# Long attention branch A: high-query by low-key products in two 64-row matmuls, one on each half of the array

## The chip, the cores and the metric

The kernel runs on one core of one Trainium2 chip. The metric is the device time of one execution in microseconds (us); lower is better. Three executions of the kernel before took 2085.16, 2086.23 and 2087.42 us (median 2086.23). TensorE is called PE for its matmuls and PEld for the loads of the stationary operand (the weights); DVE is VectorE, ACT ScalarE, POOL GpSimd, and SP is the queue from which most DMAs are issued.

## The reference, cut to what matters

One encoder layer is applied to two sequences, one of 512 tokens and one of 1024. Its token mixer has two branches. Branch A is grouped-query attention: 8 query heads of 64 values, in two groups of four heads, each group with one key and one value head:

```
def block(qi):
    s = jnp.einsum('bqkgd,bskd->bkgqs', qi, k, preferred_element_type=jnp.float32) * scale
    p = jax.nn.softmax(s, axis=-1)
    return jnp.einsum('bkgqs,bskd->bqkgd', p.astype(v.dtype), v)
```

Everything is float32: `q` and `k` are normalised and rotated before, the outputs of both branches are gated, added and multiplied by `w_out`, and an MLP follows.

## The kernel before

**Numbers in two parts.** PE multiplies values in the type `F32R`, which keeps fewer bits than float32. Every operand is therefore kept as a high part (a copy in `F32R`) and a low part (what the copy left off). A product is taken in three matmuls: high by high, low by high, high by low.

**Scores of branch A.** A head has only 64 rows to contract over, half of the array's 128. The kernel uses the other half for the low part: for an even head, `qT[0]` holds the high queries on partitions 0 to 63 and the low queries on 64 to 127; for an odd head, `qT[1]` has them the other way round. `kT[:, 0]` holds the high keys on both halves, `kT[:, 1]` the low keys on both. One matmul of `qT` (128 rows, 128 queries) with `kT[:, 0]` thus gives high by high plus low by high, and one with `kT[:, 1]` adds high by low (and low by low). A matmul covers 512 keys. The short sequence (512 tokens, `NB` = 1) needs two matmuls for a tile of 128 queries, the long one (1024 tokens, `NB` = 2) four, two for each half of the keys: lines 812 and 813, in `s_tile`.

**What follows a score tile.** DVE takes the maximum of the tile from PSUM (L815), ACT the exponential (L824), and the tile's PSUM buffer (`big`, two of them, each two banks of 512 columns) is free again. In the long sequence a head has eight tiles (`u` is head and block of 512 queries, `j` the tile in it). The block `qb` = 0 is transposed on PE (L859) and cut into high and low parts by ACT and DVE; the block `qb` = 1 is transposed by DVE, written to DRAM (`turn_a`, L878), fetched back in quarters (`fetch_a`, L903) and cut by ACT and POOL (`cut_a`). Then PE multiplies with the values (L846, L847). `fill.pull(n)` puts matmuls of the gates (`gate`, tile `gps`) between.

**Stages and order.** The short sequence comes first. For each sequence and each group `g` there is a stage phR (projections, norms, rotation; `heads_t` makes `qT` and `kT` from a transposed tile in PSUM) and a stage phA (the attention); then follow branch B, the projections, and the MLP of both sequences. For the long sequence phA runs from about 440 to 531 us (g = 0) and from 620 to 710 us (g = 1) of the profile. The code is recorded in program order, and a scheduler sets the order of each engine's instructions; the order shown below is the one that it gave.

**Buffers.** `qT`, `kT` and the values `vhl` come from one pool of equal slots of 2 x 1024 numbers for each partition; in the long sequence `vhl` fills half of its slot.

Of the kernel before, what the change touches and what calls it, by code (L numbers as in the profile page):

```python
# [18 lines left out]
P = 128  # L19
D = 1024  # L20
NC8 = D // P
HD = 64
# [39 lines left out]
def encoder(ctx: ExitStack, tc: tile.TileContext, xs, outs, w):  # L62
# [24 lines left out]
    def slot(shape, dt, name, left=False):  # L87
        return (s8l if left else s8r).tile(shape, dt, tag="s8", name=name)
# [336 lines left out]
    def run(tr, nxt, first):  # L425
# [120 lines left out]
        for g in range(2):  # L546
            with phase(f"phR{N}_{g}") as ph:
# [79 lines left out]
                    wv = load_v(g, lambda s_, d_, n_: ph.tile(s_, d_, tag="wv", name=n_, bufs=2), first and fresh, held)  # L627
                qT = [slot([P, 2, T], F32R, f"qT{N}_{g}_{i}") for i in range(2)]
                kT = slot([P, 2, T], F32R, f"kT{N}_{g}")
                vhl = slot([P, NT, P], F32R, f"vhl{N}_{g}")  # L630
                rr_of = {}

                def next_norm(tt):
# [3 lines left out]
                def heads_t(tt):  # L637
                    nm = f"{N}_{g}_{tt}"
                    pt = big(f"pq{nm}")[:, :384].rearrange("p (b q) -> p b q", q=P)
                    rrf = rr_of.pop(tt).rearrange("p h d -> p (h d)")  # L640
                    for b in range(3):
                        nc.tensor.transpose(pt[:, b, :], rrf[:, b * P : (b + 1) * P], ident)
                    ts_ = slice(tt * P, (tt + 1) * P)

                    half = (slice(0, HD), slice(HD, P))
                    nc.scalar.activation(kT[:, 0, ts_], pt[:, 2, :], AF.Copy)
                    for e in range(2):
                        op = nc.scalar.activation(qT[e][half[e], :, ts_], pt[half[e], 0:2, :], AF.Copy)
                    nc.vector.tensor_tensor(kT[:, 1, ts_], pt[:, 2, :], kT[:, 0, ts_].bitcast(F32), op=ALU.subtract)
                    for e in range(2):  # L650
                        nc.vector.tensor_tensor(
                            qT[e][half[1 - e], :, ts_],
                            pt[half[e], 0:2, :],
                            qT[e][half[e], :, ts_].bitcast(F32),
                            op=ALU.subtract,
                        )
                    return op.ins
# [142 lines left out]
            with phase(f"phA{N}_{g}") as ph:  # L800
# [3 lines left out]
                def s_tile(u, j):  # L804
                    h, qb = u
                    nm = f"{N}_{g}_{h}_{qb}_{j}"
                    q0 = (qb * 4 + j) * P
                    lhs = qT[h % 2][:, h // 2, q0 : q0 + P]
                    s = big(f"s{nm}")[:, :T]
                    for kb in range(NB):  # L810
                        ks = slice(kb * 512, kb * 512 + 512)
                        nc.tensor.matmul(s[:, ks], lhs, kT[:, 0, ks], start=True, stop=False)
                        nc.tensor.matmul(s[:, ks], lhs, kT[:, 1, ks], start=False, stop=True)  # L813
                    nm_ = sml.tile([P, 1], F32, tag="nm", name=f"nm{nm}")
                    nc.vector.tensor_reduce(nm_, s, axis=AX.X, op=ALU.max, negate=True)  # L815
                    p = ph.tile([P, T], F32, tag="P", name=f"p{nm}", bufs=8)
                    if j == 0:
                        L4[u] = ph.tile([P, 4], F32, tag="l4", name=f"l{nm}", bufs=4)
                    l = L4[u][:, j : j + 1]
                    to, of = p, s  # L820
                    if NB == 2 and qb == 1:
                        to = p.rearrange("p (b k i) -> p k b i", b=4, i=32)
                        of = s.rearrange("p (k i b) -> p k b i", b=4, i=32)
                    op = nc.scalar.activation(to, of, AF.Exp, bias=nm_, accum_out=l)  # L824
                    PP[u, j] = p
                    if j == 3:
                        rl = ph.tile([P, 32], F32, tag="r4", name=f"rl{nm}", bufs=1)
                        nc.gpsimd.memset(rl, 0.0)
                        nc.vector.reciprocal(rl[:, 0:4], L4.pop(u))
                        nc.vector.transpose(rl, rl)  # L830
                        rd[u] = dram.tile([P, 32], F32, name=f"rd{nm}")
                        nc.gpsimd.dma_start(rd[u], rl)
                    return op.ins

                o_of, rb_of = {}, {}

# [53 lines left out]
                def fetch_a(u, i):  # L890
                    nm = f"{N}_{g}_{u[0]}_{i}"
                    if i < 3:
                        hl = slot([P, 2, 16, 64], F32R, f"hq{nm}")
                        hi, lo = hl[:, 0], hl[:, 1]
                    else:
                        hi, lo = (
                            ph.tile([P, T], F32, tag="P", name=f"hq{nm}_{e}", bufs=8)
                            .bitcast(F32R)
                            .rearrange("p (a w) -> p a w", w=64)
                            for e in range(2)  # L900
                        )
                    src = PD[u].rearrange("t (a i) (b w) -> i b (t a) w", i=32, b=4)[:, :, :, 64 * i : 64 * i + 64]
                    nc.sync.dma_start(lo.bitcast(F32), src)  # L903
                    quarter[u, i] = hi, lo
# [7 lines left out]
                if NB == 2:  # L912
                    subtract[0] = nc.gpsimd
                    for u in ((0, 1), (0, 0)):
                        for j in range(4):
                            last_exp[:] = [step_s(u, j)]
                            fill.pull(1)
                    for i in range(3):
                        fetch_a((0, 1), i)
                    for h in range(4):  # L920
                        u, nn, nd = (h, 1), (h + 1, 0), (h + 1, 1)
                        for kc in range(NT):
                            t_chunk((h, 0), kc)
                            if h == 0 and kc in (0, 2, 4, 6):
                                step_s(nd, kc // 2)
                            elif 0 < h < 3 and kc in (1, 4):
                                step_s(nd, 2 + kc // 4)
                            if kc == 0 and h > 0:
                                fetch_a(u, 2)
                            if kc == 2:  # L930
                                fetch_a(u, 3)
                            if kc in (1, 2, 5):
                                cut_a(u, kc // 2)
                            fill.pull(1 if kc % 4 < 3 else 0)
                            next_pv()
                        for kc in range(NT):
                            if kc == 0:
                                cut_a(u, 3)
                            if h < 3 and kc in (0, 1, 2, 4):
                                step_s(nn, min(kc, 3))  # L940
                            if h < 2 and kc in (5, 7):
                                step_s((h + 2, 1), kc // 7)
                            hi, lo = (t[:, :, kc % 2 * 32 : kc % 2 * 32 + 32] for t in quarter[u, kc // 2])
                            queue.append((u, kc, hi, lo))
                            fill.pull(0 if kc in (1, 4) else 1)
                            next_pv()
                            if h < 3 and kc in (4, 6):
                                fetch_a(nd, kc // 2 - 2)
                else:
                    for j in range(4):  # L950
                        ends = s_tile(units[0], j)
                        last_exp[:] = [ends]
                        fill.pull(2)
                    for ui, u in enumerate(units):
                        h, qb = u
                        if first:
                            bias_row(g * 4 + ui)
                            if g == 0 and ui == 1:
                                early["a"] = load_a(1)
                            if g == 0 and ui == 2:  # L960
                                early["v"] = load_v(1, slot)
                        nxt_u = units[ui + 1] if ui + 1 < len(units) else None
                        sdone = 0
                        for kc in range(NT):
                            t_chunk(u, kc)
                            if nxt_u is not None:
                                while sdone < 4 and kc >= (0, 0, 1, 2)[sdone]:
                                    s_tile(nxt_u, sdone)
                                    sdone += 1

                            fill.pull(1)
                            next_pv()
# [1149 lines left out]
```

## Time and profile before

| what | value |
|---|---|
| time, median of three runs | 2086.23 us |
| time of the profiled execution | 2086.59 us |
| its span, first to last instruction | 2084.8 us |
| granted TensorE clock | 0.999 |
| PE busy | 2065.9 us |
| DVE busy | 1457.2 us |
| ACT busy | 1141.5 us |
| POOL busy | 449.9 us |

The profiled execution took 1.8 us more than its span. Busy times overlap, since the engines run beside each other. The end of a matmul is modelled: matmuls are pipelined, and a row's length is not the distance to the next matmul. What a stage can give up is read from the starts of matmuls that follow each other.

### The profile page before, as it was taken

What the parts mean: (1) busy time and instruction counts of PE and PEld (TensorE: products, weight loads), DVE (VectorE), ACT (ScalarE), POOL (GpSimd) and SP (SyncE); (2) the same over time, 40 slices, a digit from 0 to 9 for tenths busy, and PEclk for the clock granted to TensorE, in tenths of its full rate; (3) what the DMA queues carried; (4) which work ended last, traced back from release to release, by engine and by line L of the source; (5) the groups of instructions that cost most, each with busy time, mean ns of one, the idle gap of its engine ahead of it and who ended that gap; (6) DMA issues with size and microseconds to landing.
All of it is one profiled execution on the core that took longest, in us unless ns stands there. A gap on an engine that the chain in (4) does not pass through costs nothing. (4 is left out here: it accounts for less than half of the span.)

```text
span 2084.8 us, 31252 instructions
## 1 busy us (share of the span) xinstructions
PE 2065.9 (99%) x10615; PEld 1811.7 (87%) x10615; DVE 1457.2 (70%) x2691; ACT 1141.5 (55%) x2455; POOL 449.9 (22%) x556
## 2 busy tenths in 40 slices
PE   9999999999999999999999999999999999999998
PEld 8888878987898788888888999999999988888887
DVE  6665786778458647778845877777777777669563
ACT  6664663767557735566413665665655634334442
POOL 2324310328625744443002000011000000000000
PEclk9999999999999999999999999999999999999999
DMA  6536567558528867766544656587444899788461
GB/s 195 149 110 185 170 186 250 186 150 230 149 65 231 211 188 211 216 216 216 190 164 167 200 177 196 160 257 198 162 143 158 300 336 340 223 278 277 151 212 61
DMA packets 407910, 409.99 MB, mean 197 GB/s; under 512 B 98367, under 2 KB 334919, under 8 KB 407751
## 3 DMA queue, kind: packets, MB, share of 16 engines
q1 hardware_dynamic: 369879, 340.90, 53.0%
q10 hardware_dynamic: 27648, 40.22, 5.7%
q0 software_dynamic: 10224, 26.88, 5.1%
q8 instruction: 84, 1.38, 0.3%
q14 instruction: 75, 0.61, 0.1%
HBM read 294.21 MB, written 114.49 MB: 196 GB/s over the span
## 5 line engine op out<-in xcount | busy, mean ns | idle before, releaser
L216 PE MATMUL dn<-wd,ah 128*128 128x512 f32 x1248 | 384.2, 389 | 0.0
L216 PEld LDWEIGHTS dn<-wd,ah 128*128 128x128 f32 x1248 | 234.2, 188 | 48.7
L216 PE MATMUL dn<-wd,al 128*128 128x512 f32 x624 | 242.8, 389 | 0.0
L1596 ACT ACTIVATE ah<-ar 128x512 fp32r<-128x512 f32 x168 | 104.6, 628 | 208.6 <-PE dn L216 195.3
L216 PE MATMUL gpss<-xs_0h,w_gs 128*128 128x512 f32 x512 | 185.9, 399 | 0.0
L1597 DVE TENSOR_TENSOR al<-ar,ah 128x512 fp32r<-128x512 f32 x168 | 114.3, 686 | 81.5 <-ACT ah L1596 70.4
L216 PE MATMUL ud<-B,A 128*128 128x384 f32 x768 | 143.7, 334 | 0.7 <-DVE c L1714 0.7
L216 PE MATMUL uc<-B,A 128*128 128x384 f32 x768 | 143.7, 334 | 0.0
L216 PE MATMUL ua<-B,A 128*128 128x384 f32 x768 | 138.8, 334 | 0.0
L216 PEld LDWEIGHTS dn<-wd,al 128*128 128x128 f32 x624 | 117.1, 188 | 24.2
L216 PEld LDWEIGHTS ud<-B,A 128*128 128x128 f32 x768 | 134.0, 188 | 1.0 <-DVE c L1714 1.0
L216 PEld LDWEIGHTS uc<-B,A 128*128 128x128 f32 x768 | 134.1, 188 | 0.2 <-ACT A L1596 0.2
L216 PEld LDWEIGHTS ua<-B,A 128*128 128x128 f32 x768 | 133.7, 188 | 0.2
L180 POOL TENSOR_TENSOR rs_f<-ms_f,mhalf 128x1 f32<-128x1 f32 x6 | 4.0, 666 | 590.7 <-DVE ms_f L176 590.7
L815 DVE TENSOR_REDUCE nms<-ss 128x1 f32<-128x1024 f32 (+1 forms) x96 | 99.3, 1036 | 32.1 <-PE ss L813 31.9
L216 PE MATMUL ops<-wh_os,mgs 128*128 128x512 f32 x384 | 119.5, 391 | 0.0
L824 ACT ACTIVATE ps<-ss,nms 128x1024 f32<-128x1024 f32 (+1 forms) x96 | 93.3, 973 | 38.5 <-DVE nms L815 37.4
L216 PEld LDWEIGHTS gpss<-xs_0h,w_gs 128*128 128x128 f32 x512 | 96.1, 188 | 17.6
L216 PE MATMUL gpss<-xs_0l,w_gs 128*128 128x512 f32 x256 | 101.0, 394 | 0.0
L1227 POOL TENSOR_SCALAR pbs<-pbs,rlbs 128x384 f32<-128x384 f32 (+1 forms) x96 | 74.5, 780 | 92.8 <-DVE rlbs L1226 77.3
L1596 ACT ACTIVATE A<-S 128x512 fp32r<-128x512 f32 x128 | 75.9, 623 | 31.3 <-DVE S L1659 22.5
L216 PE MATMUL gpss<-xs_1h,w_gs 128*128 128x512 f32 x256 | 90.9, 394 | 0.0
(311 smaller groups left out, 5160.7 us busy)
## 6 DMA issues: line engine op xcount, KB each, us to landing
ar<-ud SPq DMA_DIRECT2D x120, 512.0 KB, 5.0
br<-in_w_mlp_down_dram SPq DMA_DIRECT2D x72, 512.0 KB, 5.4
rawu<-in_w_mlp_up_dram SPq DMA_DIRECT2D x64, 512.0 KB, 4.2
ud<-c ACTq DMA_DIRECT2D x128, 192.0 KB, 3.4
raw_gs<-in_w_in_dram SPq DMA_DIRECT2D x32, 512.0 KB, 3.8
tas<-ps SPq DMA_DIRECT2D x32, 512.0 KB, 2.8
hqs<-tas SPq DMA_DIRECT2D x32, 512.0 KB, 6.2
ud<-cs SPq DMA_DIRECT2D x64, 192.0 KB
```

Of the source, the lines that this page charges most:

```text
L180: op = nc.gpsimd.tensor_tensor(r[:, :n], m[:, :n], mhalf[:, :n], op=ALU.pow)
L216: op = nc.tensor.matmul(out, a, b, **kw)
L815: nc.vector.tensor_reduce(nm_, s, axis=AX.X, op=ALU.max, negate=True)
L824: op = nc.scalar.activation(to, of, AF.Exp, bias=nm_, accum_out=l)
L1227: nc.gpsimd.tensor_scalar(p, p, rl, 1.0, op0=ALU.mult, op1=ALU.mult)
L1596: nc.scalar.activation(hi, src, AF.Copy)
L1597: nc.vector.tensor_tensor(lo, src, hi.bitcast(F32), op=ALU.subtract)
```

## The change

For the long sequence alone, the two matmuls with `kT[:, 1]` contract over 64 rows instead of 128. The first takes the high queries on partitions 0 to 63 and the low keys of the first 512 there; the second takes the high queries on partitions 64 to 127 and the low keys of the last 512 there. Each writes its own PSUM bank. The product low by low is not taken any more.

The high queries are now needed on both halves. One half has them in `qT` already; a copy for the other half is kept in `qD`, in the free half of the `vhl` slot. `heads_t` fills it for heads 0 and 1 with two more ACT copies from PSUM for each tile of 128 tokens. For heads 2 and 3 it is filled later by one DMA each (`other_rows`, 64 partitions x 1024 numbers, 256 KB) from `qT`, on the SP queue, once the last score tile of head 0 or 1 has read the old rows.

```diff
@@ stage phR
-                vhl = slot([P, NT, P], F32R, f"vhl{N}_{g}")
+                if NB == 2:
+                    both = slot([P, 2, T], F32R, f"vhl{N}_{g}")
+                    vhl, qD = both[:, 0].rearrange("p (t w) -> p t w", w=P), both[:, 1]
+                else:
+                    vhl, qD = slot([P, NT, P], F32R, f"vhl{N}_{g}"), None
@@ heads_t
                     for e in range(2):
                         op = nc.scalar.activation(qT[e][half[e], :, ts_], pt[half[e], 0:2, :], AF.Copy)
+                    if qD is not None:
+                        for e in range(2):
+                            op = nc.scalar.activation(qD[half[1 - e], ts_], pt[half[e], 0, :], AF.Copy)
@@ s_tile
                         nc.tensor.matmul(s[:, ks], lhs, kT[:, 0, ks], start=True, stop=False)
-                        nc.tensor.matmul(s[:, ks], lhs, kT[:, 1, ks], start=False, stop=True)
+                        if NB == 1:
+                            nc.tensor.matmul(s[:, ks], lhs, kT[:, 1, ks], start=False, stop=True)
+                    for r in range(2 if NB == 2 else 0):
+                        rs, ks = slice(r * HD, r * HD + HD), slice(r * 512, r * 512 + 512)
+                        hi = qT[r][rs, h // 2, q0 : q0 + P] if h % 2 == r else qD[rs, q0 : q0 + P]
+                        nc.tensor.matmul(s[:, ks], hi, kT[rs, 1, ks], start=False, stop=True)
@@ stage phA
+                def other_rows(h):
+                    e = h % 2
+                    nc.sync.dma_start(
+                        qD[HD - HD * e : P - HD * e].bitcast(F32), qT[e][HD * e : HD * e + HD, h // 2].bitcast(F32)
+                    )
@@ the loop over heads, first half of a head
+                            if kc == 3 and h == 0:
+                                other_rows(2)
@@ the loop over heads, second half of a head
+                            if h == 0 and kc == 4:
+                                other_rows(3)
```

**PE, the first two score tiles of the long sequence.** `ss` is the score tile, `gps` a gate matmul, `xs` the normed input. Before:

```order
L216 MATMUL gpss_2304_0_0_5451<-xs_0h_4384,w_gs_2304_0_5278 128x512
L812 MATMUL ss_0_0_1_0_5489<-kTs_0_4598,qTs_0_0_4596 128x512
L813 MATMUL ss_0_0_1_0_5489<-kTs_0_4598,qTs_0_0_4596 128x512
L812 MATMUL ss_0_0_1_0_5489<-kTs_0_4598,qTs_0_0_4596 128x512
L813 MATMUL ss_0_0_1_0_5489<-kTs_0_4598,qTs_0_0_4596 128x512
L216 MATMUL gpss_2304_0_0_5451<-xs_0h_4384,w_gs_2304_0_5278 128x512
L216 MATMUL gpss_2304_0_0_5451<-xs_0l_4386,w_gs_2304_0_5278 128x512
L216 MATMUL gpss_2304_0_0_5451<-xs_0h_4384,w_gs_2304_0_5278 128x512
```

The same place now; L819 is the 128-row matmul with the high keys, L825 the 64-row matmul with the low keys, and `vhls` stands for `qD`, which lies in its slot:

```order
L216 MATMUL gpss_2304_0_0_5465<-xs_0h_4384,w_gs_2304_0_5288 128x512
L819 MATMUL ss_0_0_1_0_5505<-kTs_0_4598,qTs_0_0_4596 128x512 x2
L825 MATMUL ss_0_0_1_0_5505<-kTs_0_4598,qTs_0_0_4596 128x512
L825 MATMUL ss_0_0_1_0_5505<-kTs_0_4598,vhls_0_4599 128x512
L216 MATMUL gpss_2304_0_0_5465<-xs_0h_4384,w_gs_2304_0_5288 128x512
L216 MATMUL gpss_2304_0_0_5465<-xs_0l_4386,w_gs_2304_0_5288 128x512
L216 MATMUL gpss_2304_0_0_5465<-xs_0h_4384,w_gs_2304_0_5288 128x512
```

The tile has four matmuls as before, the two 128-row ones first and the two 64-row ones behind them, next to each other. So it is in 60 of the 64 tiles.

**PE, a tile whose 64-row matmuls stand apart** (head 2, first tile of block 0, now; `os` is the product with the values):

```order
L877 MATMUL pTs_0_1_0_7_6081<-ident,ps_0_1_0_3_5877 128x128
L864 MATMUL os_0_1_0_6000<-pths_0_1_0_5_6052,vhls_0_4599 128x512
L825 MATMUL ss_0_2_0_0_6095<-kTs_0_4598,qTs_0_0_4596 128x512
L865 MATMUL os_0_1_0_6000<-ptls_0_1_0_5_6053,vhls_0_4599 128x512
L825 MATMUL ss_0_2_0_0_6095<-kTs_0_4598,vhls_0_4599 128x512
L216 MATMUL gpss_2304_2_0_6110<-xs_0h_4383,w_gs_2304_2_5703 128x512
```

Here a 128-row matmul stands between the two. This is so in four tiles: this one and one of head 3, in each group.

**SP, the DMAs in the middle of phA, g = 0, now** (L849 is `other_rows`, L896 `turn_a`, L921 `fetch_a`, L512 a load of weights for the next group):

```order
L921 DMA hqs_0_0_3_1_5696<-tas_0_0_5527 128x16x64
L849 DMA vhls_0_4599<-qTs_0_0_4596 64x1024
L896 DMA tas_0_1_5692<-ps_0_1_1_1_5690 128x1024
L896 DMA tas_0_1_5692<-ps_0_1_1_2_5741 128x1024
L512 DMA rawqs_1_1_6678<-in_w_in_dram 128x4x256
L896 DMA tas_0_1_5692<-ps_0_1_1_3_5783 128x1024
L849 DMA vhls_0_4599<-qTs_0_1_4597 64x1024
L921 DMA hqs_0_1_0_5888<-tas_0_1_5692 128x16x64
```

The two rows of L849 are new, and the load L512 has moved behind one `turn_a`. Behind phA the order of PE is the same as before.

## The prediction

> **What bounds the kernel now.** I read the page's head first, then the busy times by stage, then the score tiles alone, then the starts of single matmuls.
>
> ```profile
> span 2084.8 us, 31252 instructions
> PE 2065.9 (99%) x10615; PEld 1811.7 (87%) x10615; DVE 1457.2 (70%) x2691; ACT 1141.5 (55%) x2455; POOL 449.9 (22%) x556
> 440.00:531.00 91.00, 89.90 (x434) 71.84 (x433) 75.88 (x93) 67.86 (x110) 52.21 (x57) 1.00 0.79 212
> 620.00:710.00 90.00, 90.00 (x435) 71.89 (x434) 75.45 (x93) 66.63 (x108) 52.22 (x57) 1.00 0.81 215
> 710.00:1140.00 430.00, 427.84 (x2036) 358.73 (x2036) 284.06 (x627) 207.41 (x380) 142.66 (x164) 1.00 0.64 195
> 1140.00:2060.00 920.00, 918.44 (x4705) 840.34 (x4704) 668.49 (x1046) 469.91 (x888) 33.09 (x41) 1.00 0.67 216
> ```
>
> PE is the bound everywhere. The last four rows are stretches of the span: length, then busy time of PE, PEld, DVE, ACT and POOL, granted clock, DMA share. The first two are phA of the long sequence, the only places that the edit of `s_tile` touches: PE is busy for 179.9 of 181.0 us there at full clock. The last two are what follows, with PE busy for 1346.3 of 1350. So a microsecond that PE saves in phA should arrive at the end, unless another engine makes PE wait in phA itself.
>
> A busy PE may still be a waiting one, so the next rows look at the starts:
>
> ```profile
> 440.89 0.39 PE L812 MATMUL ss<-kTs,qTs 128*128 128x512 f32 x1
> 441.12 0.39 PE L813 MATMUL ss<-kTs,qTs 128*128 128x512 f32 x1
> 441.35 0.39 PE L812 MATMUL ss<-kTs,qTs 128*128 128x512 f32 x1
> 441.57 0.39 PE L813 MATMUL ss<-kTs,qTs 128*128 128x512 f32 x1
> 441.80 0.39 PE L216 MATMUL gpss<-xs_0h,w_gs 128*128 128x512 f32 x1
> 1653.11 421.66 PE dn L216 x1860
> PEld ss L812 <- ACT ps L824: 1.9, 7, 0.4
> ```
>
> The first five are one score tile and the matmul behind it (start, length): four starts in 441.80 - 440.89 = 0.91 us. The sixth, from the chain that ended last, is the longest stream of 512-column matmuls: 421.66 / 1860 = 0.227 us from start to start. Four of those are 0.91 us, so a score tile already runs at the stream's pace, and one matmul is worth **0.227 us**, not the 0.39 of its row. The seventh, from the waits in 440:531, is what score tiles lose to a PSUM buffer that ACT hasn't freed yet: 1.9 us in that stage. PE's own pace is the limit there.
>
> **The change, part by part.**
>
> *PE: the score tiles.*
>
> ```profile
> L812 PE MATMUL ss<-kTs,qTs x64: 387/393/504, 440.9 to 531.0; 128*128 128x512 f32 x64
> L812 PE MATMUL ss<-kTs,qTs x64: 387/393/499, 620.7 to 709.6; 128*128 128x512 f32 x64
> 649.19 0.60 PE L859 MATMUL pTs<-ident,ps 128*128 128x128 f32 x4
> L859 PE MATMUL pTs<-ident,ps 128*128 128x128 f32 x384 | 59.3, 273 | 0.3 <-DVE ptls L863 0.2
> ```
>
> L812 runs twice in a tile, so 64 + 64 of it are 64 tiles. In 60 of them (the rows of order) the two 64-row matmuls are neighbours, and what the edit is worth hangs on whether they run at the same time. They use different rows of the array, different partitions of `qT`, `qD` and `kT`, and different PSUM banks, so nothing in the program's data holds the second. If it starts with the first, the pair takes one place of 0.227 us where two were: 60 x 0.227 = 13.6 us saved. If the second waits for a weights load of its own, it starts later by one load. What a load costs when nothing hides it shows in the last two rows: four transposes of 128 columns, too short to hide loads, take 0.60 us in all and one lasts 0.273, so they start (0.60 - 0.273) / 3 = 0.109 us apart. The pair then takes 0.227 + 0.109 = 0.336, and 60 x 0.118 = 7.1 us are saved. I take the middle, 0.172 us for each tile: **10.3 us**, with the ends 7.1 and 13.6. The four split tiles save nothing.
>
> The Trainium skill has a rule for this, in "TensorE: Matmul & The Clock Gate", section "Measured speedup vs the span model": matmuls on different row groups start about 4 ns apart, so that a pack lasts one matmul and 4 ns for each further tile. By it a pair saves 0.223 us, an estimate of 60 x 0.223 = 13.4 us in place of my 10.3; no run here shows such a pair.
>
> *PE: going from 128 rows to 64 and back.* Each pair that stands together is entered and left once, a split tile twice: 60 x 2 + 4 x 4 = 136 changes of shape. The rows that are nearest:
>
> ```profile
> L216 PE MATMUL dn<-wd,ah 128*128 128x512 f32 x1248 | 384.2, 389 | 0.0
> 646.79 0.50 PE L812 MATMUL ss<-kTs,qTs 128*128 128x512 f32 x1
> 647.12 0.39 PE L813 MATMUL ss<-kTs,qTs 128*128 128x512 f32 x1
> 647.35 0.40 PE L812 MATMUL ss<-kTs,qTs 128*128 128x512 f32 x1
> 646.79 0.19 PEld L812 LDWEIGHTS ss<-kTs,qTs 128*128 128x128 f32 x1 [0.31 <-ACT ps L824]
> 2.26 0.63 PE L155 MATMUL warm<-ident 128*128 128x128 f32 x2
> 2.82 0.27 PE L129 MATMUL gcol<-ident,grow 8*128 8x8 f32 x1
> ```
>
> If the array had to be empty before a change, the next matmul would start when the one before has ended and not when its stream has: 0.389 - 0.227 = 0.162 us later. If the weights load couldn't run ahead either, 0.10 us come on top: that is the difference between 647.12 - 646.79 = 0.33 us, where a load was held until the matmul's own start, and the next distance, 0.23. So a change of shape costs between 0 and 0.262 us, and 136 of them between 0 and 35.6 us; below nothing isn't possible, since a stream without changes has no stall that a change could take away. The only matmul on fewer rows in this trace is `gcol`, on 8: it starts at 2.82, while the modelled end of the full-array matmul before it is 2.26 + 0.63 = 2.89. One row, at the start and after a wait for a DMA, is little, but it is the only row of the thing itself, and it doesn't show an emptied array. I take **0** and keep the upper end for the rivals and the range.
>
> *What the other engines give back.*
>
> ```profile
> 460.00:470.00 10.00, 10.00 (x54) 8.04 (x54) 9.21 (x13) 9.94 (x16) 5.18 (x7) 1.00 0.99 238
> 490.00:500.00 10.00, 10.00 (x55) 8.18 (x54) 9.96 (x14) 8.23 (x14) 9.03 (x9) 1.00 1.08 295
> 460.00:470.00 10.00, 3.69 (x13) 2.27 (x13) 3.04 (x3) 3.38 (x6) 1.00 0.99 238
> 490.00:500.00 10.00, 2.34 (x8) 1.50 (x8) 3.62 (x3) 3.29 (x6) 1.00 1.08 295
> ```
>
> The first two rows are ten microseconds each of all work, the other two the score tiles alone in them. ACT (9.94) or DVE (9.96 of 10) is full there as well, so PE can't get ahead: the 13 + 8 matmuls, some 5 tiles, save nothing. That is 5 x 0.172 = 0.9 us, and as much in the second group: **1.8 us given back**. The bounds are 0 and the whole 10.3; over the stage as a whole DVE has 15.1 of 91 us free and ACT 23.1, so most should stay.
>
> *ACT: two more copies of 64x128 in `heads_t`,* 16 tiles, 32 copies.
>
> ```profile
> L646 ACT ACTIVATE kTs<-pqs 128x128 fp32r<-128x128 f32 x24 | 6.7, 279 | 5.6 <-PE pqs L642 5.6
> 360.00:440.00 80.00, 78.92 (x525) 74.95 (x524) 56.61 (x124) 56.58 (x213) 27.30 (x40) 1.00 0.53 162
> 439.98 0.29 DVE L649 TENSOR_TENSOR kTs<-pqs,kTs 128x128 fp32r<-128x128 f32 x1 [1.69 <-ACT qTs L648]
> ```
>
> A copy of 128 columns from the same PSUM tile takes 0.279 us: 32 x 0.279 = 8.9 us of ACT, 4.5 in a stage of 80 us in which ACT works 56.6. PE is the cover. At the stage's end the DVE cut of the low keys waits for these copies (last row) and comes up to 0.56 us later, once in each group; it would end at 439.98 + 0.29 + 0.56 = 440.83, and the first matmul with low keys is now the tile's third, at about 441.35. So 0; 1.1 us in all without that cover.
>
> *SP: four DMAs of 256 KB, two in each group.*
>
> ```profile
> vss<-vds SPq DMA_DIRECT2D x32, 256.0 KB, 3.9
> SPq L878 <- DVE ps L877: 50.0, 15, 12.8
> SPq L903 <- PE ss L813: 3.1, 3, 1.7
> 468.32 0.33 SPq L878 DMA_DIRECT2D tas<-ps  x1
> 478.58 1.53 SPq L903 DMA_DIRECT2D hqs<-tas  x2
> ```
>
> A DMA of that size lands in 3.9 us. The SP queue spends 50.0 us of 430 to 540 waiting for DVE's transposes, so the issue itself has room. `other_rows(2)` stands ahead of the `turn_a` issued at 468.32 and serves head 2; `other_rows(3)` stands ahead of the fetch at 478.58 and serves head 3, a whole head later. The second waits for the last score tile of head 1, and behind it stands the fetch of head 1's first quarters; such a wait of fetches for score matmuls is there already (3.1 us, third row). I take 0; the other end is one landing on PE's path each time, 4 x 3.9 = 15.6 us, which would need every consumer to be waiting.
>
> **The sum.** 10.3 - 1.8 = 8.5 us. Against the profiled execution: 2086.59 (span 2084.8 and 1.8 around it) - 8.5 = 2078.1. That execution lies 0.36 above the median of the three runs, so 2077.7 in their measure; I say **2078**. With the ends of the pair it is 2086.6 - 13.6 = 2073 and, with 7.1 and twice the loss, 2086.6 - 3.5 = 2083.
>
> **The rivals.**
>
> *The array is emptied at each change of shape (slower).* Place: between the second 128-row matmul and the pair, and behind the pair. Price: 136 x 0.162 = 22.0 us less 13.6 for the pair: + 8.4, **2095**. With the loads uncovered too, 35.6 - 13.6 = + 22, 2108. It decides from 13.6 / 136 = 0.10 us for a change. For it: a place of 0.162 exists between a stream's end and a matmul's end, and nothing but `gcol` has shown a change. Against it: `gcol`. The Trainium skill states this rule in "TensorEngine Tiling (Array Packing)", section "Key Properties": changing the tiling mode drains TensorE, while changing the tile does not. By that rule the time is this rival's; the trace of before has no such change inside a running stream that could confirm it.
>
> *The halves run one after the other (the change doesn't do what it says).* Each 64-row matmul takes its own 0.227 us, the tile stays at 0.91, and the time is **2087** with a little of the ACT delay. The same time comes out if a change of shape costs about 0.08 to 0.10 us and eats up what the pair saves. For it: in every row of this trace matmuls of one engine start one stream after another. Against it: the separate rows and banks.
>
> *PE saves, and another engine takes its place.* DVE or ACT fills in more stretches than I counted; with half of 10.3 lost it is 2081.5. Against it the free time above. It lies inside my forecast.
>
> **How the numbers follow.** Forecast, with its own range 2073 to 2083 and the third rival in it: 0.50. Halves in turn, or a price that cancels: 0.22. Emptied array: 0.28. Measurement can tell about 0.2% (4.2 us) from no change, so faster 0.50, same 0.22, slower 0.28. The range runs from 2072 to 2095: it takes in the forecast and the second rival and the lower half of the first; about 0.14 above and 0.02 below are left out.
>
> **What would show it.** In the changed profile: two starts of L825 next to each other a few nanoseconds apart (pair), about 0.11 apart (a load between) or 0.23 apart (in turn). The distance from the second L819 to the first L825, and from the last L825 to the next gate matmul, shows the price of a change: 0.23 for none, 0.39 for an emptied array, 0.49 with the load. A whole tile, first start to the next matmul's, now 0.91, should be 0.68 to 0.79. The stages phA should shrink by some 4 us each, PE's waits for ACT at score tiles should grow from 1.9, and L825 should never wait for a DMA. The forecast is wrong if a tile takes 0.91 or more.

## The result and the profile after

Four executions of the changed kernel took 2096.16 to 2097.12 us, median **2096.84**; four of the kernel before beside it took 2085.16 to 2087.42, median 2085.85. The ratio is 1.0051, with a 95% interval from 1.0034 to 1.0069: the changed kernel is slower, by 11 us in the medians. The forecast was 2078, its range ended at 2095.

The head of the page of the changed kernel (busy times and counts), to be read against that of before:

```profile
span 2095.1 us, 31270 instructions
...
PE 2077.5 (99%) x10615; PEld 1798.1 (86%) x10615; DVE 1458.0 (70%) x2691; ACT 1151.2 (55%) x2487; POOL 451.9 (22%) x556
```

The span is 10.3 us longer, at the same number of matmuls. PE's share says 99% as before, so it can't show what happened. The groups of the score tiles in the two stages phA show where (count, shortest / mean / longest ns, start of the first to start of the last):

```profile
L819 PE MATMUL ss<-kTs,qTs x64: 387/397/501, 443.0 to 537.1; 128*128 128x512 f32 x64
L825 PE MATMUL ss<-kTs,qTs x32: 491/498/502, 443.6 to 537.5; 64*128 64x512 f32 x32
...
L819 PE MATMUL ss<-kTs,qTs x64: 387/396/501, 627.0 to 721.1; 128*128 128x512 f32 x64
L825 PE MATMUL ss<-kTs,qTs x32: 491/498/502, 627.5 to 721.5; 64*128 64x512 f32 x32
```

From the first to the last matmul with high keys it was 440.9 to 531.0 and 620.7 to 709.6, that is 90.1 + 88.9 = 179.0 us. Now it is 94.1 + 94.1 = 188.2: **9.2 us more, in these two stretches**. The rest of the 10.3 is 2.1 us ahead of the first score tile, 0.2 between the groups and 1.2 us less behind the second; experiment 1, with the same copies and DMAs, and experiment 3, without them but with its first score tile as late (442.85), put that down as scatter. The second thing to see is the length of L825: a 64-row matmul takes 0.49 to 0.50 us in every record, where a 128-row one that runs in a stream takes 0.39.

The timeline of PE in the changed kernel, the first two score tiles of the long sequence (start, length; an x2 row holds two matmuls):

```profile
442.79 0.39 PE L216 MATMUL gpss<-xs_0h,w_gs 128*128 128x512 f32 x1
443.02 0.61 PE L819 MATMUL ss<-kTs,qTs 128*128 128x512 f32 x2
443.56 0.50 PE L825 MATMUL ss<-kTs,qTs 64*128 64x512 f32 x1
443.56 0.50 PE L825 MATMUL ss<-kTs,vhls 64*128 64x512 f32 x1
443.99 0.50 PE L216 MATMUL gpss<-xs_0h,w_gs 128*128 128x512 f32 x1
444.33 0.39 PE L216 MATMUL gpss<-xs_0l,w_gs 128*128 128x512 f32 x1
444.56 0.40 PE L216 MATMUL gpss<-xs_0h,w_gs 128*128 128x512 f32 x1
444.80 0.62 PE L819 MATMUL ss<-kTs,qTs 128*128 128x512 f32 x2
```

The two L825 start at the same 443.56: **the pair does run at once**. But look at the distances around it. The second L819 starts 0.61 - 0.39 = 0.22 behind the first, at 443.24; from it to the pair are 0.32 us, from the pair to the next 128-row matmul 0.43, and from that one to the following 0.34, where a stream has 0.227 each time; behind that it is 0.23 again. From the second L819 to 444.33 it is 1.09 us, where three places of the stream are 0.68. So going to 64 rows and back costs **0.41 us**, and the pair saves one place of 0.227.

The weights loads in the same place (the bracket is the idle time of the loader before the row, and what ended it):

```profile
442.79 0.41 PEld L819 LDWEIGHTS ss<-kTs,qTs 128*128 128x128 f32 x2
443.56 0.18 PEld L825 LDWEIGHTS ss<-kTs,qTs 64*128 64x128 f32 x1 [0.35 <-issue]
443.56 0.18 PEld L825 LDWEIGHTS ss<-kTs,vhls 64*128 64x128 f32 x1
443.99 0.19 PEld L216 LDWEIGHTS gpss<-xs_0h,w_gs 128*128 128x128 f32 x1 [0.24 <-issue]
444.10 0.19 PEld L216 LDWEIGHTS gpss<-xs_0l,w_gs 128*128 128x128 f32 x1
```

They split the 0.41. In a stream a load runs while the matmul before it streams: the load of the gate matmul of 444.33 starts at 444.10, 0.23 ahead of it. The loads of the pair, and of the first 128-row matmul behind it, start only with their own matmul (443.56, 443.99). That is why L825 lasts 0.50 instead of 0.39 (the 128-row matmul at 646.79 of before, whose load was held by a wait, lasts 0.50 too and has 0.33 behind it), and it puts 0.11 on the distance *behind* such a matmul: 0.34 = 0.227 + 0.11, and 0.43 = 0.227 + 0.11 + 0.10. What is left is 0.32 - 0.227 = 0.09 on the way in and 0.10 on the way out, a gap in which neither a load nor a matmul starts. **A change of shape thus costs some 0.10 us in which nothing starts and 0.11 us of a load that doesn't run ahead, about 0.20 together.**

The waits between 430 and 545 us of the changed kernel (engine, tile and line, what it waited for, us in total, times, longest):

```profile
PEld ss L825 <- issue: 11.7, 34, 0.4
...
PEld ss L819 <- ACT ps L836: 0.5, 2, 0.3
...
SPq L849 <- PE ss L825: 4.5, 1, 4.5
SPq L849 <- PE pTs L877: 2.4, 1, 2.4
```

All 34 ways into 64 rows of this group (30 pairs and 4 that stand apart) hold the loader, for 11.7 / 34 = 0.34 us. PE's wait for ACT at score tiles, 1.9 before, has shrunk to 0.5. The two new DMAs wait on their queue for PE, and no row has L825 waiting for a DMA.

All distances of the two stretches, from the first to the last score matmul, give the full account. Each distance is taken less what a matmul has in a stream (0.227 us for 512 columns, 0.108 for 128):

| us, both groups | before | after |
|---|---|---|
| from a 128-row matmul to a 64-row one | | 7.0 |
| from a 64-row one to a 128-row one | | 13.2 |
| behind the first 128-row one | | 6.2 |
| the second matmul of 60 pairs | | -13.4 |
| all other gaps of PE | 7.2 | 3.5 |

The three upper rows are 26.4 us for 134 changes, 0.197 each (the last of the 136, one in each group, lie behind the last score matmul). The pairs save 13.4, 0.224 each. Of the 13.0 us that are left, 3.6 hide in gaps that PE had before, waits for ACT among them: + 9.4 us.

### The profile page after: what moved, and what is told of

Its sections match the earlier page's. It is cut to its first block, busy times and chain, and to the rows that moved or that the text cites. A ratio compares the mean times of both kernels' runs of the same rounds, so it can differ in the third digit from the quotient of the medians.

```text
span 2095.1 us, 31270 instructions
## 1 busy us (share of the span) xinstructions
PE 2077.5 (99%) x10615; PEld 1798.1 (86%) x10615; DVE 1458.0 (70%) x2691; ACT 1151.2 (55%) x2487; POOL 451.9 (22%) x556
## 4 chain that ended last, share of the span: by engine, by line
PE 77%; DVE 1%; issue 1%; ACT 1%; DMA 1%; POOL 0%; SPq 0%; POOLq 0%; ACTq 0%; DVEq 0%
PE dn L216 20%; PE gpss L216 8%; PE ua L216 6%; PE ud L216 6%; PE uc L216 6%; PE ops L216 4%; PE ub L216 3%; PE zs L216 2%; PE ppbs L216 2%; PE pqbs L216 2%; PE pkbs L216 2%; PE zvs L216 2%; PE ppas L216 2%; PE os L864 2%; PE dnf L216 2%; PE ss L819 1%
## 5 line engine op out<-in xcount | busy, mean ns | idle before, releaser
L1618 ACT ACTIVATE ah<-ar 128x512 fp32r<-128x512 f32 x168 | 104.5, 628 | 206.9 <-PE dn L216 188.2
```

The source lines that it names most:

```text
L1618: nc.scalar.activation(hi, src, AF.Copy)
```

## The experiments

**Theory:** every change between 128 and 64 rows costs about 0.20 us, and nothing else of the edit costs anything. **Rivals:** the copies, the DMAs or the new order cost it; two matmuls at once disturb each other; any matmul on fewer than 128 rows pays, whether or not the array is divided.

Lengths in the table are from the first to the last score matmul, both groups together. A pair counts where its two matmuls start together; each saves 0.224 us.

| run | changes of shape | pairs | score stretches, us | against before |
|---|---|---|---|---|
| before | 0 | 0 | 179.5 | |
| side work only | 0 | 0 | 178.9 | -0.6 |
| 96 rows | 0 | 0 | 179.1 | -0.4 |
| half the tiles | 64 | 32 | 183.0 | +3.5 |
| the change | 136 | 60 | 188.9 | +9.4 |
| both on one half | 136 | 0 | 202.5 | +23.0 |
| 64-row matmuls apart | 256 | 0 | 225.4 | +45.9 |
| two pairs in a tile | 156 | 120 | 179.8 | +0.3 |
| two tiles at a time | 72 | 62 | 192.1 | +12.6 |

At 0.20 us for a change, less 0.224 for each pair and less the 2 to 5 us that hide in other gaps of PE, every row with 64-row matmuls comes out but the last; experiment 6 says why the last does not.

**1. The side work alone.** The changed kernel with the score matmuls of before; the copies, `qD` and the DMAs stay.

```diff
-                        if NB == 1:
-                            nc.tensor.matmul(s[:, ks], lhs, kT[:, 1, ks], start=False, stop=True)
-                    for r in range(2 if NB == 2 else 0):
-                        ...
+                        nc.tensor.matmul(s[:, ks], lhs, kT[:, 1, ks], start=False, stop=True)
```

> The changed kernel with the four 128-row matmuls of before; the copies into qD, its place in the vhl slot and the four DMAs stay. Theory 'change of shape' (each passage of PE between 128 and 64 rows costs about 0.20 us: 0.09 for emptying the array, 0.11 for a weights load that can't run ahead): 2086, within 2 us of before, since no shape changes. Rival 'contention' (two 64-row streams at once slow each other, the pair takes 0.43 us): 2086 as well. Rival 'side work' (the ACT copies and DMAs are what costs): about 2096.

Measured: 2087.93 us in ten executions, ratio 1.0003 [0.9993, 1.0012]. Its score groups:

```profile
L819 PE MATMUL ss<-kTs,qTs x64: 387/393/501, 442.6 to 531.7; 128*128 128x512 f32 x64
...
L819 PE MATMUL ss<-kTs,qTs x64: 387/393/504, 621.3 to 710.7; 128*128 128x512 f32 x64
```

89.1 + 89.4 = 178.5 us, where the same rows of before have 179.0. The first score tile starts at 442.6, nearly as late as in the changed kernel, and yet the whole isn't measurably longer: the 2 us ahead of it aren't the change's price. The rival of the side work falls.

**2. Both 64-row matmuls on the same half.** From the kernel before; they follow each other behind the two 128-row ones, and nothing can run at once.

```diff
-                        nc.tensor.matmul(s[:, ks], lhs, kT[:, 1, ks], start=False, stop=True)
+                    for kb in range(NB if NB == 2 else 0):
+                        rs, ks = slice(h % 2 * HD, h % 2 * HD + HD), slice(kb * 512, kb * 512 + 512)
+                        nc.tensor.matmul(s[:, ks], lhs[rs], kT[rs, 1, ks], start=False, stop=True)
```

> The kernel before, with the two low-key matmuls of the long sequence cut to the 64 rows on which the high queries already lie (both on the same half; low by low is left out; no qD, no copies, no DMAs). 'Change of shape': two changes for each of 64 tiles and no place saved, 64 x 0.40 = 25.6 us, so about 2111; the distance into the first is 0.32, out of the last 0.43. 'Contention': no two streams run at once, so 2086. 'Side work': 2086.

Measured: 2110.89 us, ratio 1.0108 [1.0093, 1.0123]. The timeline of its first tile:

```profile
440.90 0.61 PE L812 MATMUL ss<-kTs,qTs 128*128 128x512 f32 x2
441.45 0.73 PE L817 MATMUL ss<-kTs,qTs 64*128 64x512 f32 x2
442.11 0.50 PE L216 MATMUL gpss<-xs_0h,w_gs 128*128 128x512 f32 x1
442.44 0.40 PE L216 MATMUL gpss<-xs_0l,w_gs 128*128 128x512 f32 x1
```

From the first L812 to 442.44 it is 1.54 us for five matmuls, which have 1.14 in a stream: 0.40 more, the same price as around a pair, with nothing running at once and no copy or DMA added. Matmuls disturbing each other are not needed to explain it. By the account above the changes cost 26.6 us, and 3.6 of it hides in PE's other gaps. They are 136 and not the 128 of the expectation, since in four tiles the scheduler put a 128-row matmul between the two.

**3. The 64-row matmuls apart.** As experiment 2, but in the order of before, so that every one lies between two 128-row matmuls.

```diff
-                        nc.tensor.matmul(s[:, ks], lhs, kT[:, 1, ks], start=False, stop=True)
+                        rs = slice(h % 2 * HD, h % 2 * HD + HD) if NB == 2 else slice(0, P)
+                        nc.tensor.matmul(s[:, ks], lhs[rs], kT[rs, 1, ks], start=False, stop=True)
```

> As e2, but each 64-row matmul stands right behind the 128-row one of its key half, so that they are apart (low by low is left out). 'Change of shape': four changes for each tile, 64 x 0.80 = 51 us, so about 2137, and twice the loss of e2. 'Contention' and 'side work': 2086.

Measured: 2134.06 us, ratio 1.0226 [1.0211, 1.0241]. The timeline:

```profile
442.85 0.39 PE L812 MATMUL ss<-kTs,qTs 128*128 128x512 f32 x1
443.17 0.50 PE L814 MATMUL ss<-kTs,qTs 64*128 64x512 f32 x1
443.60 0.49 PE L812 MATMUL ss<-kTs,qTs 128*128 128x512 f32 x1
444.02 0.50 PE L814 MATMUL ss<-kTs,qTs 64*128 64x512 f32 x1
444.45 0.50 PE L216 MATMUL gpss<-xs_0h,w_gs 128*128 128x512 f32 x1
444.78 0.39 PE L216 MATMUL gpss<-xs_0l,w_gs 128*128 128x512 f32 x1
```

Five distances, 1.93 us where a stream has 1.14: 0.79 for two ways in and out. Twice as many changes as in experiment 2 cost twice as much (51.2 against 26.6 us by the account). Again some 5 us hide in other gaps, which the expectation had left out.

**4. A pair for the high keys as well.** The changed kernel with high by high taken in a pair too, right before the pair with the low keys: four matmuls in two places, for one way in and out. Low queries by high keys are not taken.

```diff
-                        nc.tensor.matmul(s[:, ks], lhs, kT[:, 0, ks], start=True, stop=False)
-                        ...
+                    for i in range(2 if NB == 2 else 0):
+                        for r in range(2):
+                            ...
+                            nc.tensor.matmul(s[:, ks], hi, kT[rs, i, ks], start=i == 0, stop=i == 1)
```

> The changed kernel with the high-key products as a pair of 64-row matmuls too (low queries by high keys and low by low are left out), so two pairs follow each other in a tile. 'Change of shape': two changes as in the changed kernel and one place of 0.227 less, 2097 - 14.5 = 2082, with 2 us given back perhaps; the second pair starts 0.23 us behind the first. 'Contention': each pair takes 0.43, so the tile is as long as in the changed kernel, 2097, and the pairs start 0.43 apart.

Measured: 2088.97 us, ratio 1.0005 [0.9996, 1.0015]. A miss: the gain didn't come. Its second tile, first PE and then the loads:

```profile
447.33 0.50 PE L825 MATMUL ss<-kTs,qTs 64*128 64x512 f32 x1
447.33 0.50 PE L825 MATMUL ss<-kTs,vhls 64*128 64x512 f32 x1
447.67 0.39 PE L825 MATMUL ss<-kTs,qTs 64*128 64x512 f32 x1
447.67 0.39 PE L825 MATMUL ss<-kTs,vhls 64*128 64x512 f32 x1
448.00 0.50 PE L216 MATMUL gpss<-xs_0h,w_gs 128*128 128x512 f32 x1
448.34 0.40 PE L216 MATMUL gpss<-xs_0l,w_gs 128*128 128x512 f32 x1
```

```profile
447.33 0.18 PEld L825 LDWEIGHTS ss<-kTs,qTs 64*128 64x128 f32 x1 [0.36 <-issue]
447.33 0.18 PEld L825 LDWEIGHTS ss<-kTs,vhls 64*128 64x128 f32 x1
447.44 0.19 PEld L825 LDWEIGHTS ss<-kTs,qTs 64*128 64x128 f32 x1
447.44 0.19 PEld L825 LDWEIGHTS ss<-kTs,vhls 64*128 64x128 f32 x1
447.99 0.19 PEld L216 LDWEIGHTS gpss<-xs_0h,w_gs 128*128 128x128 f32 x1 [0.37 <-issue]
```

This takes the price apart. The loads of the second pair do run ahead (447.44, for a start at 447.67), so the second pair lasts 0.39 and the way out is 0.33 = 0.227 + 0.10: the gap alone. What is held is a load across a change, not a load of 64 rows. The gain is missing for a reason in the order: the scheduler put other matmuls between, and there are 78 ways into 64 rows instead of 64. The 14 more are 14 x 0.41 = 5.7 us, and 8 of the 128 pairs stand apart, 8 x 0.224 = 1.8; that is about the 7 us by which the expectation was missed. By the account the ways cost some 31 us and the pairs save 27, and 4 us hide in other gaps.

**5. 96 rows.** The kernel before with 96 of 128 rows for the low keys; for odd heads, part of the high queries by low keys is missing.

```diff
-                        nc.tensor.matmul(s[:, ks], lhs, kT[:, 1, ks], start=False, stop=True)
+                        rs = slice(0, 96) if NB == 2 else slice(0, P)
+                        nc.tensor.matmul(s[:, ks], lhs[rs], kT[rs, 1, ks], start=False, stop=True)
```

> As the kernel before, but the low-key matmuls of the long sequence contract over partitions 0 to 95 instead of all 128 (part of the low queries by low keys, and for odd heads part of the high queries by low keys, is left out); order and count of matmuls as before, 128 and 96 rows in turn. 'Change of shape', if it hangs on how the array is divided: 96 rows need the undivided array, nothing changes, 2087 and 0.91 us for a tile. If it hangs on any change in the number of rows: four changes for each tile, 64 x 0.80 = 51 us as in e3, about 2135.

Measured: 2089.05 us, ratio 1.0008 [0.9999, 1.0018]. The timeline:

```profile
441.08 0.39 PE L812 MATMUL ss<-kTs,qTs 128*128 128x512 f32 x1
441.30 0.40 PE L814 MATMUL ss<-kTs,qTs 96*128 96x512 f32 x1
441.54 0.40 PE L812 MATMUL ss<-kTs,qTs 128*128 128x512 f32 x1
441.77 0.40 PE L814 MATMUL ss<-kTs,qTs 96*128 96x512 f32 x1
442.01 0.40 PE L216 MATMUL gpss<-xs_0h,w_gs 128*128 128x512 f32 x1
```

Distances of 0.22 to 0.24 and no length of 0.50 in these rows: going from 128 to 96 rows and back is free. The price doesn't come with any smaller number of rows: 64 have it and 96 don't. No experiment has a count between them or below 64.

**6. Two tiles at a time.** The changed kernel with four 128-row matmuls for two tiles first and then both pairs, so that two pairs share one way in and out.

```diff
+                        tiles = [(j - 1, s_mm(u, j - 1)), (j, s_mm(u, j))]
+                        with tc.issue_after(last_f[-1]):
+                            for jj, s in tiles:
+                                s_low(u, jj, s)
```

(`s_mm` has the matmuls with high keys, `s_low` the pair.)

> The changed kernel with its score tiles taken two at a time: four 128-row matmuls, then both pairs; 28 groups of two pairs stay whole, and PE leaves the 128-row shape 36 times instead of 68. 'Change of shape' (0.40 us for each time it is left): 32 x 0.40 = 12.8 us less than the changed kernel, 2084 to 2086, about the time of before, since two places of 0.227 pay for 0.40 with 0.05 left. If two tiles at once leave no PSUM buffer free and PE then waits for DVE and ACT: up to 10 us more, 2096. If the price is for each 64-row matmul and not for each change: as the changed kernel, 2097.

Measured: 2102.23 us, ratio 1.0077 [1.006, 1.0094], slower than the change itself. Its waits between 435 and 545 us:

```profile
PEld ss L834 <- ACT ps L861: 8.0, 10, 2.9
...
PE ss L834 <- ACT ps L861: 4.4, 3, 2.4
```

The longest of them on PE, in its timeline:

```profile
456.65 0.73 PE L834 MATMUL ss<-kTs,qTs 128*128 128x512 f32 x2 [2.43 <-ACT ps L861]
```

The changes fell to 36 ways in and out. But there are two PSUM buffers for score tiles: two tiles at once take both, and PE stands until ACT has read the first, once in each group for 2.4 us where the longest such wait of before was 0.4. By the account, with these two waits counted for themselves, the 36 ways cost 15 us, 0.42 each, where the change pays 26.4: the saving is real. But the two waits are 5 us, and PE's other gaps in the stretches grew to 14.3 us, where they shrank to 2 to 5 in every other run with 64-row matmuls. The new waits are dearer.

**7. Pairs in half of the tiles.** The changed kernel with pairs for `j` = 0 and 2 alone.

```diff
-                        if NB == 1:
+                        if NB == 1 or j % 2:
                             nc.tensor.matmul(s[:, ks], lhs, kT[:, 1, ks], start=False, stop=True)
-                    for r in range(2 if NB == 2 else 0):
+                    for r in range(2 if NB == 2 and j % 2 == 0 else 0):
```

> The changed kernel with the pair in every second score tile (j = 0 and 2); the other tiles take four 128-row matmuls as before. The copies and the four DMAs stay. Nothing of the computation is left out but low by low in the tiles with a pair. By its order 32 pairs stand together and none apart, so PE goes into 64-row matmuls and back 32 times, against 68 in the changed kernel. Theory (each going and coming costs 0.40 us and a pair saves 0.227): 32 x 0.173 = 5.5 us over the kernel before, about 2091.5, and half of what the changed kernel loses; the two stages phA at about 118.5 us each, halfway between 116 and 121. Rival (the loss is made once in a stage, by the new order or a buffer that comes free late, not at each change): 2086 to 2087 if the tiles without a pair mend it, or 2096 to 2097 if it stays whole.

Measured: 2091.8 us in eleven executions, 4.7 above the 2087.09 of before beside it, ratio 1.0021 [1.0012, 1.003]. Its waits between 430 and 545 us:

```profile
PEld ss L825 <- issue: 5.7, 16, 0.4
...
PEld ss L819 <- ACT ps L836: 1.1, 4, 0.4
```

16 held loads in a group instead of 34, and a loss between nothing and that of the change, at neither of the rival's times: the loss goes with the number of changes. By the account 32 ways in and out cost 13.0 us, 0.41 each, the pairs save 7.2, and 2.4 hide in other gaps; the stretches grow by 3.5 us. The stages as the expectation counts them, from the first score tile to the work behind phA, are 118.0 and 117.6 us long, against 116.7 and 115.6 before and 120.9 and 121.1 with the change.

No run of the study beat the kernel before.

## Why the prediction was wrong

**What bounds the kernel: right.** PE's pace arrives at the end: 9.4 us were lost in the score stretches, and 11 in the medians of the whole; the difference is no larger than the scatter of what lies outside them.

**The pair: right, under-sized.** The second matmul starts with the first. I took 0.172 us a pair, the middle between a load of its own and none; the runs have 0.224, 13.4 us in all against 10.3. The Trainium skill's rule in "TensorE: Matmul & The Clock Gate", section "Measured speedup vs the span model" (about 4 ns for each further tile), gave an estimate of 13.4, and the trace agrees: the 60 pairs start 3 to 4 ns apart.

**The step that failed: "I take 0" for 136 changes of shape.** They cost 0.197 us each, 26.4 us in the two stretches. The bounds of 0 and 0.262 were right; the choice between them hung on one row, `gcol`, which couldn't decide it. I compared its start, 2.82, with the modelled end of the matmul before it, 2.89, and read it as no sign of an emptied array. The changed kernel shows that such an overlap is no sign of a free change: the pair starts at 443.56, and the second L819 ends by its row at 443.02 + 0.61 = 443.63; the gate matmul starts at 443.99, and the pair ends at 443.56 + 0.50 = 444.06. The overlap is 0.07 us each time, and each time a gap has been paid, since in a stream the next start lies 0.389 - 0.227 = 0.16 ahead of that end: 0.16 - 0.07 = 0.09.

That `gcol` has the same 0.07 doesn't make it a sample of the price either. Two rows of the trace of before, PE and its loader:

```profile
1.35 1.54 PE L155 MATMUL warm<-ident 128*128 128x128 f32 x6 [1.35 <-POOL ident masks.py:199]
2.82 0.18 PEld L129 LDWEIGHTS gcol<-ident,grow 8*128 8x128 f32 x1 [0.33 <-DMA grow<-in_norm_mix_g_dram]
```

The load of `gcol` waited for a DMA and started with its matmul, so the DMA set that start. And the matmuls ahead of it ran at about half the pace: the first starts at 1.35, the fifth at 2.26, 0.23 us apart where 128 columns take 0.109 later. So the trace of before had no row of a change inside a running stream, and the 0 had no row to stand on. The middle of the bounds, which I took for the pair, would have been 136 x 0.131 = 17.8 us, more than the pairs can save.

The prediction's own sign of being wrong came: the first tile takes 443.99 - 443.02 = 0.97 us, more than 0.91.

**The first rival: right in mechanism and direction.** Its price was 0.162, from the same modelled end, and 0.262 with the loads uncovered. Measured are 0.09 to 0.10 for the gap and 0.11 for the load: the first smaller than I had it, the second as I had it, and both are paid. Its two sums, 2095 and 2108, enclose the time. The Trainium skill has the rule in "TensorEngine Tiling (Array Packing)", section "Key Properties": changing the tiling mode drains TensorE. The trace agrees, in so far as nothing starts for that gap around every change to the half array and back (experiments 2, 3 and 7) and there is none for 96 rows (experiment 5); the profile itself names no cause for the gap ("issue").

**What the other engines give back: wrong sign, small.** I took 1.8 us off the gain, because PE can't run ahead of DVE and ACT. As PE got slower, it worked the other way: 3.6 us of the loss hide in gaps that PE had anyway, and the wait for ACT fell from 1.9 to 0.5 us instead of growing.

**Side work: right.** The copies and the DMAs cost nothing that can be measured (experiment 1).

**Halves in turn: wrong.** Its second form, a price of 0.08 to 0.10 for a change that cancels the gain, had one half of the price.

Left open: whether the gap and the held load depend on the length of the stream or on the columns used, since every 64-row matmul here has 512 columns and full output. What it would take to bring experiment 4 or 6 below the kernel before wasn't tried; with two pairs for each way in and out the margin is 2 x 0.224 - 0.41 = 0.04 us, by this estimate 1 us in all for the 32 groups of experiment 6 and 2.4 for the 64 tiles of experiment 4.

## What to carry to other kernels

Packing two half-array matmuls saves one place of the stream, and going to the half array and back costs 1.8 such places here: by these figures at least two packs must follow each other without a full-array matmul between to pay at all, a gain that no run here reached; so count the ways in and out in the scheduler's order before counting the pairs. When a single row is the only sample of a mechanism, look first at what its start waited for; then compare it with what an ordinary row does by the same measure, here the start of the next matmul against the modelled end, before reading it as a no. Where several tiles are gathered to save changes, look first at how many buffers they hold at once.

## What the runs showed of the hardware

- A matmul on 96 rows between 128-row matmuls costs nothing (distances 0.22 to 0.24 us); on 64 rows it costs 0.40 to 0.41 us for the way in and out, alone or as a pair (experiments 2 and 3, the change).
- Within 64 rows, loads run ahead as usual (447.44 for a start at 447.67, on rows that a matmul is using), and the loads of the two halves start together (447.44 both, experiment 4). Across a change they don't run ahead (443.56 and 443.99 in the change).
- Behind a change of shape the next matmul started 0.07 us ahead of the modelled end of the one before (443.56 against 443.63), in a stream 0.16 ahead. A start ahead of the modelled end doesn't show that a change was free.
